# A decoder block in fp32r: stationary operands read with a step of two elements

## The chip, the cores and the metric

The kernel runs on one core of a Trainium2 chip. The metric is the device time of one execution in microseconds. The profiler's record of one execution is read as the page and as answers from the trace; the engines are TensorE (PE, its weight loads PEld), VectorE (DVE), ScalarE (ACT), GpSimd (POOL) and the queue engine SP.

## The reference

One layer on x of 256 tokens by 2048 channels, batch 1:

```python
proj = x @ w_in                       # 2048 -> q, k, v, gates of two branches
o = gla_chunked(q, k, v, log_a)       # gated linear attention, 4 heads
y_gla = (rms(o) * gla_norm_g * silu(gr)) @ w_branch_gla
y_fox = fox_attention(fq, fk, fv, log_f) @ w_branch_fox   # 8 heads
x = layer_norm(ALPHA * x + (sigmoid(ma) * y_gla + sigmoid(mb) * y_fox) @ w_out)
h = gelu(causal_dwconv(x @ w_gate, conv_w, conv_b)) * (x @ w_up)      # 2048 -> 5632
x = layer_norm(ALPHA * x + h @ w_down)
x = x + sigmoid(x @ w_ple_gate) * (p @ w_ple_proj)
```

Everything is float32. The large products are done in fp32r, each from three partial products of a high and a low part.

## The kernel before

**Operands.** Weights come from memory in units of 128 partitions by 2048 floats. `prep` splits each half of a unit: ACT copies it to an fp32r tile `hi` (line 121), DVE subtracts that from the raw values into `lo` (line 241). Activations are kept transposed, channels on partitions, as tiles of four K tiles by 512 columns: 256 columns high part, then 256 low part, each with the 256 tokens in two halves of 128 (`xT`, `x1T`, `x2T`, `oT`, `ofT`, `mC`, `hC`). Sums of activations for Strassen-like products (`xS`, `mS`, `hS`, `gS`) are cells of 128 high and 128 low columns.

**Two kinds of matmul.** In a *weight unit* (`w_unit`, lines 307 and 309; `w_phase`, lines 322 and 326) 128 columns of the weight are stationary and the activation streams: 512 columns against `hi`, then 256 against `lo`. The outputs `psg`, `psu`, `psq` and so on have channels on partitions. Elsewhere 128 tokens of an activation are stationary and 512 columns of weights stream: `fv` (line 472), `x_mm` (line 353), `q_unit` (line 979, for `psm`, `psa`, `psb`), `s_half` (lines 841 and 909, for `gv`, `gr`, `wo`, `dn`, `pg`). Each matmul loads its own stationary operand. `go` (line 1084) multiplies attention weights `ath`, `atl` as stationary by values `vh`, `vl`; transposes use `ident`.

**Order.** Instructions of SP are issued in the written order, and PE's at three places; the rest is ordered by the scheduler from its cost estimates. Weight units are prepared up to three ahead. Side work (attention steps, sums, differences of weights stored for later as `td`) is pulled in between units by generators. SBUF pools are laid out one behind the other, with paddings `GAPS` between them and a shift `LO_SHIFT` of 16 floats of the `lo` tiles in all units outside `UA`; the change leaves these as they are.

Of the kernel before, what the change touches and what calls it, by code (L numbers as in the profile page):

```python
# [78 lines left out]
def tile_block(ctx: ExitStack, tc: tile.TileContext, wu, wfv, wpp, xT_in, x_in, pT_in, wlr,  # L79
# [219 lines left out]

    def w_unit(ps, hi, lo, act, kts, first, last, hoff=0, tick=None):  # L300


        n = len(kts)
        for i, kt in enumerate(kts):
            a = act[kt // 4]
            w0 = (hoff + i) * P
            nc.tensor.matmul(ps, lhsT=hi[i // 8 if hoff == 0 else 0][:, w0 % 1024:w0 % 1024 + P],  # L307
                             rhs=a[:, kt % 4, :], start=first and i == 0, stop=False)
            nc.tensor.matmul(ps[:, 256:512],  # L309
                             lhsT=lo[i // 8 if hoff == 0 else 0][:, w0 % 1024:w0 % 1024 + P],  # L310
                             rhs=a[:, kt % 4, 0:256], start=False, stop=last and i == n - 1)
            if tick is not None:
                tick(i)

    def w_phase(ps, hi, lo, act, t, kts, part=slice(None)):


        p4 = ps.rearrange("p (s t n) -> p s t n", s=2, t=2)
        for kt in kts[part]:
            a = act[kt // 4][:, kt % 4, :]  # L320
            w = slice(kt % 8 * P, kt % 8 * P + P)
            nc.tensor.matmul(p4[:, :, t, :], lhsT=hi[kt // 8][:, w],
                             rhs=a.rearrange("p (s t n) -> p s t n", s=2, t=2)[:, :, t, :],
                             start=t == 0 and kt == kts[0], stop=False)
            if t == 1:
                nc.tensor.matmul(ps[:, 256:512], lhsT=lo[kt // 8][:, w], rhs=a[:, 0:256],
                                 start=False, stop=kt == kts[-1])

    def comb(ps, o, scale=1.0):
        tmp = t1("tmp")  # L330
        copy(tmp, ps[:, 256:512], scale)
        a = ps[:, 0:256]
        if len(o.shape) == 3:
            a, tmp = [v.rearrange("p (t n) -> p t n", t=2) for v in (a, tmp)]
        if scale == 1.0:
            nc.vector.tensor_tensor(o, a, tmp, ALU.add)
        else:
            nc.vector.scalar_tensor_tensor(o, a, scale, tmp, ALU.mult, ALU.add)

    def x_mm(banks, w, a, toks, first, last, cs=(0, 1), part=None):  # L340
# [117 lines left out]
    for u in range(8):  # L458
        hi, lo = fvu[u]
        for j in range(2):  # L460
            kt = 2 * u + j
            a = xT[kt // 4][:, kt % 4, :]
            prods = [[(hi[j], a[:, t * P:t * P + P]), (hi[j], a[:, 256 + t * P:256 + t * P + P]),
                      (lo[j], a[:, t * P:t * P + P])] for t in range(2)]
            if u < 2:
# [118 lines left out]
    def fox_gen():  # L584
# [40 lines left out]
        def values(h):  # L625
# [6 lines left out]
            dst = ofT[h // 4][:, h % 4, :]  # L632
            copy(dst[:, 0:256], po[:, 0:256])
            nc.vector.tensor_tensor(dst[:, 256:512], po[:, 0:256],
                                    dst[:, 0:256].bitcast(F32), ALU.subtract)

# [15 lines left out]
    for n in range(16):  # L652
# [6 lines left out]
        if n % 8 == 0:  # L659
            fqk[h // 4] = s8([P, 4, 2, 256], name=f"fqk{h // 4}")  # L660
        comb(ps, fqk[h // 4][:, h % 4, j], (P ** -0.5, 1.0)[j])
        if n >= 1:
# [124 lines left out]
    def cell(o, i):  # L787

        return o[:, i, 0:P], o[:, i, P:256]

    def s_sums(y):

        a11, a21, a12, a22 = [y[:, k, t * P:t * P + P] for k in range(2) for t in range(2)]
        v = t2("sums").rearrange("p (i t) -> p i t", t=P)
# [5 lines left out]
    def sums(y, name, scale=1.0, full=False):  # L800
# [7 lines left out]
        for e, src in parts:  # L808
            copy(o[:, e, 0:P], src, scale)
            hi = o[:, e, 0:P].bitcast(F32)  # L810
            if scale == 1.0:
                nc.vector.tensor_tensor(o[:, e, P:256], src, hi, ALU.subtract)
            else:
                nc.vector.scalar_tensor_tensor(o[:, e, P:256], src, scale, hi, ALU.mult,
                                               ALU.subtract)
# [110 lines left out]
    def x_sums(pairs):  # L926
        for i, pair in pairs:
# [19 lines left out]
            nc.sync.dma_start(y, xT_in[:, 2 * pair:2 * pair + 2, :])  # L947
            v = s_sums(y)
            for j, w in enumerate(ws):
                src = v[:, j * m:j * m + m]  # L950
                copy(w[:, :, 0:P], src)
                nc.vector.tensor_tensor(w[:, :, P:256], src, w[:, :, 0:P].bitcast(F32),
                                        ALU.subtract)
            yield

    def x_cl(pair, j, t):
        kt = 2 * pair + j
        a = xT[kt // 4][:, kt % 4, :]
        return a[:, t * P:t * P + P], a[:, 256 + t * P:256 + t * P + P]

    def x_st(pair, i):
        if i < 3:
            return x_cl(pair, (0, 1, 1)[i], (0, 0, 1)[i])
        o = xS[pair][i - 3]
        return o[:, 0:P], o[:, P:256]


    def q_unit(ps, act, k, first, last, tick=None):
# [4 lines left out]
        def part(i, t):  # L973
            kt = 4 * k + i
            o = act[kt // 4][:, kt % 4, :]
            ah, al = o[:, t * P:t * P + P], o[:, 256 + t * P:256 + t * P + P]
            h, l = [w[i // 2][:, i % 2 * 512:i % 2 * 512 + 512] for w in (hi, lo)]
# [137 lines left out]

    def split_T(pt, dst, t):

        p3 = pt.rearrange("p (k t) -> p k t", t=P)
        hi = dst[:, :, t * P:t * P + P]
        copy(hi, p3)  # L1120
        nc.vector.tensor_tensor(dst[:, :, 256 + t * P:256 + t * P + P], p3,
                                hi.bitcast(F32), ALU.subtract)

# [18 lines left out]
    def turn_pair(pair):  # L1142
# [19 lines left out]
        nc.vector.scalar_tensor_tensor(dst[:, :, 256:512], p3, 0.5,  # L1162
                                       dst[:, :, 0:256].bitcast(F32), ALU.mult, ALU.subtract)

# [23 lines left out]
    def ln_steps(zof, stats, t, act_out, gb_, cg, cb, nm, prio, aff):  # L1188
# [29 lines left out]
        def turn(g):  # L1218
            zc = zof(t, g)
            with tc.high_priority(prio):  # L1220
# [3 lines left out]
                if g in aff:  # L1224
                    split_T(pt, act_out[g], t)
                    return
                y = t2("lny").rearrange("p (k t) -> p k t", t=P)
                for i in range(4):
# [5 lines left out]
                    else:  # L1234
                        nc.vector.tensor_scalar(y[:, i, :], src, gc, bc, ALU.mult, ALU.add)
                hi = act_out[g][:, :, t * P:t * P + P]
                copy(hi, y)
                nc.vector.tensor_tensor(act_out[g][:, :, 256 + t * P:256 + t * P + P], y,
                                        hi.bitcast(F32), ALU.subtract)

        return stat, norm, turn

    def out_proj(nh, tail, mid, end=None):
        def cl(pair, j, t):
# [3 lines left out]
            a = mC[i // 2][:, i % 2 * 2 + j, :]  # L1248
            return a[:, t * P:t * P + P], a[:, 256 + t * P:256 + t * P + P]

# [169 lines left out]
    for n in range(NF):  # L1420
# [30 lines left out]
        dst = hC[n // 4][:, n % 4, :]  # L1451
        copy(dst[:, 0:256], h)
        nc.vector.tensor_tensor(dst[:, 256:512], h, dst[:, 0:256].bitcast(F32), ALU.subtract)
        if pair in DN_S[0] and j == 1:
            v = s_sums(yp)
            for i in range(2):
                w = sm.tile([P, 2, 256], F32R, tag="t2", bufs=6, name="hs")
                copy(w[:, :, 0:P], v[:, 2 * i:2 * i + 2])
                nc.vector.tensor_tensor(w[:, :, P:256], v[:, 2 * i:2 * i + 2],
                                        w[:, :, 0:P].bitcast(F32), ALU.subtract)  # L1460
                k = DN_S[0].index(pair)
# [26 lines left out]
    def down(nh, tail, mid):  # L1488
        def cl(pair, j, t):
            a = hC[pair // 2][:, pair % 2 * 2 + j, :]  # L1490
            return a[:, t * P:t * P + P], a[:, 256 + t * P:256 + t * P + P]

# [106 lines left out]
    def g_cl(pair, j, t):  # L1599
        kt = 2 * pair + j  # L1600
        a = x2T[kt // 4][:, kt % 4, :]
        return a[:, t * P:t * P + P], a[:, 256 + t * P:256 + t * P + P]

    gS_ = {}

    def g_sums(pairs):
        two = s8([P, 8, 256], F32R, name=f"gS{pairs[0]}")
        for i, pair in enumerate(pairs):
# [3 lines left out]
            nc.vector.tensor_tensor(y, a[:, :, 0:256], a[:, :, 256:512], ALU.add)  # L1612
            v = s_sums(y)
            copy(o[:, :, 0:P], v)
            nc.vector.tensor_tensor(o[:, :, P:256], v, o[:, :, 0:P].bitcast(F32), ALU.subtract)
            gS_[pair] = o
# [38 lines left out]
def _wst(w):  # L1655

    k, n = w.shape
    kt, nt = k // P, n // P
    per = 2048 // (kt * P)
# [32 lines left out]
def _fold(a):  # L1692

    return np.concatenate([a[:P], a[P:][::-1]], 0)


# [4 lines left out]
def _layout(i):  # L1701
# [26 lines left out]
    for lev in range(1, 8):  # L1728
# [4 lines left out]
    cmask = np.concatenate([caus.T, caus], 1)  # L1733
    return dict(wu=wu, wfv=wfv, wpp=_xst(i["w_ple_proj"][0]), xT=x.T.reshape(16, P, S).transpose(1, 0, 2),
                x=x.reshape(2, P, D), pT=_fold(i["p"][0, 0]).T.reshape(2, P, S).transpose(1, 0, 2),
                wlr=i["w_gla_lr"][0], chan=chan, gnorm=i["gla_norm_g"], lng=lng,
# [21 lines left out]
```

## Time and profile before

| | |
|---|---|
| median of 3 runs | 1645.58 us (1645.08 to 1645.61) |
| span of the profiled execution | 1645.0 us |
| PE busy | 1638.4 us, 8,422 matmuls |
| PEld busy | 1404.3 us |
| DVE busy | 1356.0 us, 1,964 instructions |
| ACT busy | 910.3 us, 1,277 instructions |
| moved by DMA | 477.81 MB, 290 GB/s |

The profiled execution has no time of its own beside its span; the runs' median stands 0.6 us above that span. In the page a row of a group reads: line, engine, operation, output<-inputs, shapes, count | busy us, mean ns of one | idle us of the engine before them and what ended it. In a timeline a row is: start in us, duration in us, engine, line, operation, count. In a table of windows it is the busy time of each engine with the number of its instructions, the granted TensorE clock, the busy share of the DMA engines and GB/s. A row of one line's instructions gives count, the minimum, median and maximum of a duration in ns, and the first and last start.

### The profile page before, as it was taken

The numbers are of one execution on the slowest core, as the hardware profiler recorded it, in microseconds if no ns is written. First come the engines' busy times: TensorE is split into PE (matmuls) and PEld (weight loads), VectorE is DVE, ScalarE is ACT, GpSimd is POOL, SyncE is SP. The second block draws the span as 40 slices with busy tenths as digits, with TensorE's granted clock in tenths as the row PEclk, the third lists the DMA queues.
The fourth block names the chain that finished last, engine by engine and source line by source line (L and its number), as shares of the span: only waits on it lengthen the run. The fifth ranks groups of instructions, "written<-read, shape, count | busy, mean of one in ns | idle before, by whom it ended". The sixth has DMA issues, their size and how long they took to land.

```text
span 1645.0 us, 23490 instructions
## 1 busy us (share of the span) xinstructions
PE 1638.4 (100%) x8422; PEld 1404.3 (85%) x8422; DVE 1356.0 (82%) x1964; ACT 910.3 (55%) x1277; POOL 92.7 (6%) x244
## 2 busy tenths in 40 slices
PE   9999999999999999999999999999999999999998
PEld 9988888888888888887898888888888888888887
DVE  7687899788989867778987888887887778988887
ACT  6655555456666654446574445555455456566554
POOL 0000000000000000000010111110111000000000
PEclk9999999999999999999999999999999999999999
DMA  8799799878888768889855898888766679899574
GB/s 324 281 371 341 290 383 356 294 258 309 306 333 307 252 207 303 305 335 364 296 190 194 315 338 320 308 306 304 279 239 217 210 260 336 305 343 348 177 258 157
DMA packets 114838, 477.81 MB, mean 290 GB/s; under 512 B 13032, under 2 KB 14320, under 8 KB 95136
## 3 DMA queue, kind: packets, MB, share of 16 engines
q1 hardware_dynamic: 105216, 417.57, 70.8%
q0 software_dynamic: 9504, 58.73, 8.9%
q8 instruction: 66, 1.08, 0.2%
q14 instruction: 52, 0.43, 0.1%
HBM read 417.53 MB, written 58.73 MB: 290 GB/s over the span
## 4 chain that ended last, share of the span: by engine, by line
PE 97%; DMA 1%; DVE 1%; ACT 0%; issue 0%; POOL 0%; ACTq 0%
PE psm L979 11%; PE dn L841 10%; PE psu L307 10%; PE psg L307 9%; PE psa L979 5%; PE psu L309 5%; PE psg L309 5%; PE dn_p L841 4%; PE gr L841 3%; PE gv L841 3%; PE fv L472 3%; PE pg L353 3%; PE psb L979 3%; PE wo L841 2%; PE gr_p L841 2%; PE gv_p L841 2%
## 5 line engine op out<-in xcount | busy, mean ns | idle before, releaser
L241 DVE TENSOR_TENSOR lo<-raw,hi 128x1024 fp32r<-128x1024 f32 x456 | 551.1, 1220 | 140.7 <-ACT hi L121 139.4
L121 ACT ACTIVATE hi<-raw 128x1024 fp32r<-128x1024 f32 x456 | 476.6, 1057 | 304.2 <-DMA raw<-in_wu_dram 83.7
L307 PE MATMUL psu<-x1T,hi 128*128 128x512 f32 x688 | 240.4, 392 | 0.0
L307 PE MATMUL psg<-x1T,hi 128*128 128x512 f32 x672 | 234.8, 392 | 0.0
L309 PE MATMUL psu<-x1T,lo 128*128 128x256 f32 x688 | 192.3, 280 | 0.0
L309 PE MATMUL psg<-x1T,lo 128*128 128x256 f32 x672 | 187.8, 280 | 0.0
L979 PE MATMUL psm<-hi,xT 128*128 128x512 f32 x512 | 163.0, 392 | 0.0
L307 PEld LDWEIGHTS psu<-x1T,hi 128*128 128x128 f32 x688 | 129.2, 188 | 27.6
L307 PEld LDWEIGHTS psg<-x1T,hi 128*128 128x128 f32 x672 | 126.2, 188 | 27.0
L309 PEld LDWEIGHTS psu<-x1T,lo 128*128 128x128 f32 x688 | 130.6, 190 | 0.0
L121 ACT ACTIVATE hi_b<-raw 128x512 fp32r<-128x512 f32 x112 | 92.9, 841 | 66.8 <-DMA raw<-in_wu_dram 17.9
L309 PEld LDWEIGHTS psg<-x1T,lo 128*128 128x128 f32 x672 | 127.6, 190 | 0.0
L159 DVE TENSOR_TENSOR td<-td 128x512 f32<-128x512 f32 x172 | 117.6, 684 | 0.9
L215 DVE TENSOR_TENSOR lo_b<-raw,hi_b 128x512 fp32r<-128x512 f32 x112 | 104.9, 952 | 15.9 <-ACT hi_b L121 15.6
L979 PEld LDWEIGHTS psm<-hi,xT 128*128 128x128 f32 x512 | 96.2, 188 | 19.6
L215 DVE TENSOR_TENSOR lo_t<-td,hi_t 128x1024 fp32r<-128x1024 f32 x86 | 101.7, 1219 | 12.7 <-ACT hi_t L121 12.0
L121 ACT ACTIVATE hi_t<-td 128x1024 fp32r<-128x1024 f32 x86 | 88.0, 1053 | 28.9 <-DMA td<-td 15.1
L979 PE MATMUL psm<-lo,xT 128*128 128x512 f32 x256 | 99.8, 390 | 0.0
L841 PE MATMUL dn<-hi,hC 128*128 128x512 f32 x352 | 97.8, 389 | 0.0
L979 PE MATMUL psa<-hi,oT 128*128 128x512 f32 x256 | 81.2, 392 | 0.0
L841 PEld LDWEIGHTS dn<-hi,hC 128*128 128x128 f32 x352 | 66.0, 188 | 13.7
L979 PEld LDWEIGHTS psa<-hi,oT 128*128 128x128 f32 x256 | 48.1, 188 | 10.0
(414 smaller groups left out, 3130.8 us busy)
## 6 DMA issues: line engine op xcount, KB each, us to landing
raw<-in_wu_dram SPq DMA_DIRECT2D x525, 512.0 KB, 6.3
td<-in_wu_dram SPq DMA_DIRECT2D x43, 1024.0 KB, 8.8
td<-td POOLq DMA_DIRECT2D x43, 1024.0 KB, 7.7
td<-td SPq DMA_DIRECT2D x43, 1024.0 KB, 8.3
hS<-sd SPq DMA_DIRECT2D x11, 1024.0 KB, 8.8
raw<-in_wu_dram SPq DMA_DIRECT2D x43, 256.0 KB, 7.7
fvraw<-in_wfv_dram SPq DMA_DIRECT2D x13, 524.0 KB, 6.6
sd<-hs POOLq DMA_DIRECT2D x24, 256.0 KB, 5.6
```

The source lines that it names most:

```text
L121: return nc.scalar.activation(o, i, AF.Copy, bias=0.0, scale=scale)
L159: sub = lambda o, a, b: nc.vector.tensor_tensor(o, a, b, ALU.subtract)
L215: nc.vector.tensor_tensor(lo, src, hi.bitcast(F32), ALU.subtract)
L241: i = nc.vector.tensor_tensor(lo, raw, hi.bitcast(F32), ALU.subtract)
L307: nc.tensor.matmul(ps, lhsT=hi[i // 8 if hoff == 0 else 0][:, w0 % 1024:w0 % 1024 + P], rhs=a[:, kt % 4, :], start=first and i == 0, stop= ...
L309: nc.tensor.matmul(ps[:, 256:512], lhsT=lo[i // 8 if hoff == 0 else 0][:, w0 % 1024:w0 % 1024 + P], rhs=a[:, kt % 4, 0:256], start=False, ...
L353: nc.tensor.matmul(bs[j][:, 0:m], lhsT=x, rhs=v[:, o:o + m], start=first and i == 0, stop=last and i == 2)
L472: nc.tensor.matmul(fbk[t][c][:, 0:n], lhsT=x, rhs=w[:, o:o + n], start=kt == 0 and i == 0, stop=kt == 15 and i == 2)
L841: nc.tensor.matmul(ps[:, e], lhsT=x, rhs=w, start=k == 1, stop=k == total.get(id(ps), 3 * ns))
L979: nc.tensor.matmul(ps[t], lhsT=x, rhs=v, start=first and i == 0 and j == 0, stop=last and i == 3 and j == 2)
```

## The change

All fp32r stationary operands but those of `go`, of the gates' low-rank product and of a sum over partitions are read with a step of two elements, 8 bytes. For that, data are laid out anew:

- Weight units: the host writes two K tiles in turn, element by element (`_wst`); `wcols` reads every second column.
- Activations: the two token halves stand in turn, element by element, in the high and in the low part (`tok`, `by_half`). The host does it for `x` and `p` (`_mix`); elsewhere ACT and DVE write with a step of two (`put_T`, `hC`, `mC`, `ofT`). `x1T`, which only streams, keeps its order.
- Cells: the high and the low value of a token stand side by side (`cell`, `cells`).
- Where a tile in the new order streams, its products come out with tokens in that order; `comb` then reads PSUM by halves.
- The split of an `mC` pair is done in two instructions on ACT and two on DVE, not one each.

```diff
+    def tok(a, s, t):
+
+        return a.rearrange("p (s n t) -> p s t n", s=2, t=2)[:, s, t, :]
+
+    def by_half(v):
+
+        return v.rearrange("p (n t) -> p t n", t=2)
...
+    def wcols(w, kt):
+
+        v = w[kt // 8].rearrange("p (k n j) -> p k j n", n=P, j=2)
+        return v[:, kt % 8 // 2, kt % 2, :]
...
-            nc.tensor.matmul(ps, lhsT=hi[i // 8 if hoff == 0 else 0][:, w0 % 1024:w0 % 1024 + P],
-                             rhs=a[:, kt % 4, :], start=first and i == 0, stop=False)
...
+            nc.tensor.matmul(ps, lhsT=wcols(hi, i), rhs=a[:, kt % 4, :],
+                             start=first and i == 0, stop=False)
+            nc.tensor.matmul(ps[:, 256:512], lhsT=wcols(lo, i), rhs=a[:, kt % 4, 0:256],
+                             start=False, stop=last and i == n - 1)
...
-            a, tmp = [v.rearrange("p (t n) -> p t n", t=2) for v in (a, tmp)]
+            a, tmp = by_half(a), by_half(tmp)
...
-            ah = a[:, t * P:t * P + P]
-            al = a[:, 256 + t * P:256 + t * P + P]
+            ah, al = tok(a, 0, t), tok(a, 1, t)
...
     def cell(o, i):
 
-        return o[:, i, 0:P], o[:, i, P:256]
...
+        v = o[:, i, :].rearrange("p (n j) -> p j n", j=2)
+        return v[:, 0, :], v[:, 1, :]
...
+    def put_T(src, dst, t, mixed):
+
+        if mixed:
+            hi, lo = [dst.rearrange("p k (s n t) -> p s t k n", s=2, t=2)[:, i, t] for i in range(2)]
+        else:
+            hi, lo = [dst[:, :, o + t * P:o + t * P + P] for o in (0, 256)]
+        copy(hi, src)
+        nc.vector.tensor_tensor(lo, src, hi.bitcast(F32), ALU.subtract)
...
-        dst = mC[i // 2][:, i % 2 * 2:i % 2 * 2 + 2, :]
-        copy(dst[:, :, 0:256], p3, 0.5)
-        nc.vector.scalar_tensor_tensor(dst[:, :, 256:512], p3, 0.5,
-                                       dst[:, :, 0:256].bitcast(F32), ALU.mult, ALU.subtract)
+        for k in range(2):
+            dst = mC[i // 2][:, i % 2 * 2 + k, :]
+            hi, lo = by_half(dst[:, 0:256]), by_half(dst[:, 256:512])
+            src = p3[:, k, :].rearrange("p (t n) -> p t n", t=2)
+            copy(hi, src, 0.5)
+            nc.vector.scalar_tensor_tensor(lo, src, 0.5, hi.bitcast(F32), ALU.mult, ALU.subtract)
...
-    a = w.reshape(kt, P, nt // per, per, P).transpose(2, 1, 3, 0, 4)
-    return a.reshape(nt // per, P, 2048)
+    a = w.reshape(k // 256, 2, P, n // P, P).transpose(3, 2, 0, 4, 1)
+    return a.reshape(n // P, P, k)
...
+def _mix(a):
+
+    return a.reshape(-1, 2, P).transpose(0, 2, 1).reshape(a.shape)
```

The numbers of instructions on PE, POOL and SP stay; DVE and ACT have three more each. Order changes at one place, the start of `wo`. ACT before (`mC` from the turned tiles `mt` of pairs 6 and 7, among the splits of unit 122):

```order
L121 ACTIVATE hi122_b2_6991<-raw122_1_6982 128x1024
L121 ACTIVATE mC0_6213<-mt6_7027 128x2x256
L121 ACTIVATE mC1_7039<-mt7_7034 128x2x256
L121 ACTIVATE hi122_t13_6995<-td122_6985 128x1024
L121 ACTIVATE hi122_t24_6999<-td122_6985 128x1024
```

ACT now:

```order
L129 ACTIVATE hi122_b2_6993<-raw122_1_6984 128x1024
L129 ACTIVATE mC0_6213<-mt6_7029 128x2x128
L129 ACTIVATE mC1_7043<-mt7_7038 128x2x128
L129 ACTIVATE hi122_t13_6997<-td122_6987 128x1024
L129 ACTIVATE mC0_6213<-mt6_7029 128x2x128
L129 ACTIVATE hi122_t24_7001<-td122_6987 128x1024
L129 ACTIVATE mC1_7043<-mt7_7038 128x2x128
```

The second halves of the two splits stand behind the copies of unit 122. PE before (products p5, p7, p6 of unit 121, one row of three each; p6 and p7 take the two banks that `mt` and other turned tiles use):

```order
L841 MATMUL wo0_p5_6980<-hi121_t13_6928,mS1_6269 128x512
L841 MATMUL wo0_p7_7067<-hi121_t13_6928,mS1_6269 128x512
L841 MATMUL wo0_p7_7067<-lo121_t13_6929,mS1_6269 128x512
L841 MATMUL wo0_p7_7067<-hi121_t13_6928,mS1_6269 128x512
L841 MATMUL wo0_p6_7066<-hi121_t24_6932,mS1_6269 128x512
L841 MATMUL wo0_p6_7066<-lo121_t24_6933,mS1_6269 128x512
L841 MATMUL wo0_p6_7066<-hi121_t24_6932,mS1_6269 128x512
L841 MATMUL wo0_10_6977<-hi121_t24_6932,mS1_6269 128x512
```

PE now, from the last of unit 121's other products on:

```order
L858 MATMUL wo0_10_6979<-hi121_t24_6934,mS1_6271 128x512
L858 MATMUL wo0_p1_6981<-hi122_b11_6989,mS3_6551 128x512
L858 MATMUL wo0_p1_6981<-lo122_b11_6990,mS3_6551 128x512
L858 MATMUL wo0_p1_6981<-hi122_b11_6989,mS3_6551 128x512
L858 MATMUL wo0_00_6977<-hi122_b2_6993,mS3_6551 128x512
L858 MATMUL wo0_00_6977<-lo122_b2_6994,mS3_6551 128x512
L858 MATMUL wo0_00_6977<-hi122_b2_6993,mS3_6551 128x512
L858 MATMUL wo0_01_6978<-hi122_b2_6993,mS3_6551 128x512
L858 MATMUL wo0_p7_7073<-hi121_t13_6930,mS1_6271 128x512
L858 MATMUL wo0_p7_7073<-lo121_t13_6931,mS1_6271 128x512
```

The six matmuls of p7 and p6 of unit 121 now stand behind seven matmuls of unit 122, and, with them, three of product 10 that need other banks.

More of the change, by code (lines that the diff above doesn't have):

```diff
@@ L297, in load_consts2, with w_unit @@
             nc.gpsimd.tensor_copy(mask[:, 4 * i:4 * i + 4, :], maskf)
-    def w_unit(ps, hi, lo, act, kts, first, last, hoff=0, tick=None):
+    def wcols(w, kt):
+        v = w[kt // 8].rearrange("p (k n j) -> p k j n", n=P, j=2)
+        return v[:, kt % 8 // 2, kt % 2, :]
+    def w_unit(ps, hi, lo, act, kts, first, last, tick=None):
         n = len(kts)
@@ L462, in tile_block @@
             a = xT[kt // 4][:, kt % 4, :]
-            prods = [[(hi[j], a[:, t * P:t * P + P]), (hi[j], a[:, 256 + t * P:256 + t * P + P]),
-                      (lo[j], a[:, t * P:t * P + P])] for t in range(2)]
+            prods = [[(hi[j], tok(a, 0, t)), (hi[j], tok(a, 1, t)), (lo[j], tok(a, 0, t))]
+                     for t in range(2)]
             if u < 2:
@@ L787, in cell, with cells, s_sums @@
     def cell(o, i):
-        return o[:, i, 0:P], o[:, i, P:256]
-    def s_sums(y):
-        a11, a21, a12, a22 = [y[:, k, t * P:t * P + P] for k in range(2) for t in range(2)]
+        v = o[:, i, :].rearrange("p (n j) -> p j n", j=2)
+        return v[:, 0, :], v[:, 1, :]
+    def cells(o):
+        v = o.rearrange("p i (n j) -> p j i n", j=2)
+        return v[:, 0], v[:, 1]
+    def s_sums(y, mixed=False):
+        h = y.rearrange("p k (n t) -> p k t n" if mixed else "p k (t n) -> p k t n", t=2)
+        a11, a21, a12, a22 = [h[:, k, t] for k in range(2) for t in range(2)]
         v = t2("sums").rearrange("p (i t) -> p i t", t=P)
@@ L1601, in g_cl @@
         a = x2T[kt // 4][:, kt % 4, :]
[L1602 removed]
+        return tok(a, 0, t), tok(a, 1, t)
     gS_ = {}
```

86 lines of the change are left out of this document (38 added, 48 removed).

## The prediction

> **What bounds the kernel now.** I read the page first: busy times, granted clock, the chain that ended last.
>
> ```profile
> span 1645.0 us, 23490 instructions
> PE 1638.4 (100%) x8422; PEld 1404.3 (85%) x8422; DVE 1356.0 (82%) x1964; ACT 910.3 (55%) x1277; POOL 92.7 (6%) x244
> ...
> PEclk9999999999999999999999999999999999999999
> ...
> PE 97%; DMA 1%; DVE 1%; ACT 0%; issue 0%; POOL 0%; ACTq 0%
> ```
>
> The reader is to see that TensorE never lacks work at a full granted clock. The list of waits, for PE alone, confirms it; this is its whole answer:
>
> ```profile
> PE warm_ps L131 <- DVE warm L128: 1.2, 1, 1.2
> PE wo L841 <- DVE lo_b L215: 0.4, 1, 0.4
> PE wo_p L841 <- ACT hi_t L121: 0.2, 1, 0.2
> ```
>
> So the time is what 8,422 matmuls take back to back, and the question is what one costs. A matmul's own record overlaps the next one's, so I take distances between starts, from the timeline of PE. First the gate units, which alternate 512 and 256 columns (first rows, and the row twelve pairs later):
>
> ```profile
> 999.81 0.28 PE L309 MATMUL psg<-x1T,lo 128*128 128x256 f32 x1
> 999.93 0.39 PE L307 MATMUL psg<-x1T,hi 128*128 128x512 f32 x1
> ...
> 1003.97 0.28 PE L309 MATMUL psg<-x1T,lo 128*128 128x256 f32 x1
> ```
>
> 4.16 us / 12 = 346.7 ns a pair. Then a merge gate, 512 columns only (first row, and the row twelve matmuls later):
>
> ```profile
> 300.21 0.39 PE L979 MATMUL psm<-lo,xT 128*128 128x512 f32 x1
> ...
> 302.93 0.39 PE L979 MATMUL psm<-lo,xT 128*128 128x512 f32 x1
> ```
>
> 2.72 / 12 = 226.7 ns. The 256-column matmul therefore takes 346.7 - 226.7 = 120.0 ns, so 256 more columns cost 106.7 ns, 0.4167 ns each; 512 columns stream in 213.3 ns, and **13.3 ns of every matmul do not depend on its columns**. That is the sum at stake. A third place has the same form, 512 columns, with stationary and moving operands from other tiles (first row, and the row six matmuls later):
>
> ```profile
> 584.39 0.39 PE L1084 MATMUL go<-vh,ath 128*128 128x512 f32 x1
> ...
> 585.79 0.39 PE L1084 MATMUL go<-vh,ath 128*128 128x512 f32 x1
> ```
>
> 1.40 / 6 = 233.3 ns: here the surplus is 20.0 ns. Same type, same columns, same clock; what differs is where the operands lie. In the kernel's own allocation the next stationary starts 256 bytes (modulo 512) past the moving operand in nearly all 512-column matmuls, and 320 bytes past it in these. So at least 6.7 ns of such a surplus belong to the addresses that the weight load and the stream read at the same time.
>
> **The change, part by part.** Of the matmuls, 8,010 get a stationary with step two (counted in the built program); the 251 fp32 ones, the 36 of `go` and 16 others keep step one. Columns, count, DMAs and SP's and POOL's rows stay.
>
> (1) The load and the stream. The stream covers 4 bytes in 0.4167 ns, 9.6 bytes/ns. The load's own rate is seen where nothing else limits it, in transposes of 128 columns:
>
> ```profile
> 552.97 1.03 PE L1102 MATMUL gt<-ident,og 128*128 128x128 f32 x8
> ...
> L1102 PE MATMUL gt<-ident,og 128*128 128x128 f32 x32 | 4.1, 272 | 0.0
> L307 PEld LDWEIGHTS psg<-x1T,hi 128*128 128x128 f32 x672 | 126.2, 188 | 27.0
> L309 PEld LDWEIGHTS psg<-x1T,lo 128*128 128x128 f32 x672 | 127.6, 190 | 0.0
> ```
>
> (1.03 - 0.272) / 7 = 108 ns for 128 columns, 4.7 bytes/ns with step one: half the stream's pace. So the stream overtakes the load once in a while, and if both come to the same part of the memory, one must wait. With step two the load walks at 9.5 bytes/ns, the stream's pace: a distance that is free of meetings at the start stays free. The trace has no load with step two, so the gain is bounded: above by the whole 13.3 ns (8,010 x 13.3 = 106.8 us), below by nothing or a loss (rivals). The nearest row is that of `go`: 6.7 ns hang on addresses there, 53.4 us if that much goes. I take the middle of 6.7 and 13.3, 10 ns, since the usual placement may still contain meetings that no placement with step one avoids: **-80.1 us**. [...]
>
> (2) VectorE and ScalarE write and read activations with step two. Line 718 has steps of two elements at its lowest level (one of seven) and runs at the others, so its spread holds the price; line 728 is plain, and line 713 is the same case on ACT:
>
> ```profile
> L718 DVE TENSOR_TENSOR kq<-gk,e x28: 408/416/426, 188.0 to 365.3; 128x256 f32<-128x256 f32 x28
> ...
> L728 DVE TENSOR_TENSOR kq<-gq,e 128x256 f32<-128x256 f32 x4 | 1.7, 417 | 0.0
> ...
> L713 ACT ACTIVATE e<-e x28: 399/418/449, 186.9 to 364.5; 128x256 f32<-128x256 f32 x28
> ```
>
> 416 against 417 ns on DVE, and at most 31 ns over the median on ACT: nothing that counts from SBUF. Reading PSUM with step two (32 combines of q and k) is not in the trace; between nothing and a doubling of this row's 419 ns (13 us of DVE in all) I take nothing, as the SBUF rows do, and keep 5 us for the range, since DVE idles little there:
>
> ```profile
> L338 DVE SCALAR_TENSOR_TENSOR gq<-psq,tmp 128x256 f32<-128x256 f32 x8 | 3.4, 419 | 3.2 <-ACT tmp L121 3.2
> ```
>
> (3) Three `mC` splits become six. On DVE 683 ns become 2 x 419 (the row above has the half size), half a microsecond in all; ACT is as little. But at the start of `wo` ACT's second halves now stand behind two `hi_t` copies:
>
> ```profile
> L1162 DVE SCALAR_TENSOR_TENSOR mC<-mt,mC x3: 680/683/683, 651.1 to 747.1; 128x512 fp32r<-128x512 f32 x3
> ...
> 745.24 1.07 ACT L121 ACTIVATE mC<-mt 128x512 fp32r<-128x512 f32 x2
> 746.20 2.07 ACT L121 ACTIVATE hi_t<-td 128x1024 fp32r<-128x1024 f32 x2
> ```
>
> The bank that `mt` holds comes free about 2 us later, and products p6 and p7 wait for such a bank. PE has seven matmuls moved ahead of them (7 x 0.227 = 1.6 us) as cover. Between 0 and 2 us; I take **+1**.
>
> (4) What a faster TensorE runs into. DVE, ACT and DMA keep their work; in 41-us windows:
>
> ```profile
> core 0: us, PE busy (x) PEld busy (x) DVE busy (x) ACT busy (x) POOL busy (x), PEclk, DMA share, GB/s
> 82.00:123.00 41.00, 41.00 (x243) 36.47 (x242) 36.61 (x66) 22.06 (x42) 2.13 (x4) 1.00 0.99 372
> 205.00:246.00 41.00, 41.00 (x247) 36.58 (x246) 38.91 (x63) 20.23 (x32) 2.13 (x4) 1.00 0.99 387
> 738.00:779.00 41.00, 40.32 (x180) 32.45 (x179) 36.48 (x41) 27.12 (x32) 0.53 (x1) 1.00 0.98 367
> 779.00:820.00 41.00, 41.00 (x182) 33.95 (x181) 39.42 (x48) 21.60 (x22) 0.53 (x1) 1.00 0.85 310
> ...
> L241 DVE TENSOR_TENSOR lo<-raw,hi 128x1024 fp32r<-128x1024 f32 x456 | 551.1, 1220 | 140.7 <-ACT hi L121 139.4
> ```
>
> At 5% less, a window has 39 us. Three have DMA at 0.98 or more: if none of them shrinks, 3 x 2 = 6 us come back. In the last one DVE alone needs 39.4 us, and its splits also wait for ACT; I give such windows 4 us. Late next are thus the splits and the transfers: **+10**.
>
> **Sum.** 1645.0 - 80.1 + 1 + 10 = 1575.9 us of span; the runs' median, 1645.58, stands 0.6 above the span. So 1576.5, rounded to 1577.
>
> **Rivals.**
> (a) *No effect.* The 13.3 ns are a fixed turn of the array from one stationary to the next, and step one and two load alike: 1646. Against it: 233.3 beside 226.7 ns. For it: only a placement was varied there, never the step. [...]
> (b) *More meetings, slower.* A load with step two covers 1,024 bytes instead of 512. If each stretch that it reads costs the stream as much as now, the surplus doubles: 8,010 x 13.3 = +107, 1752. It decides as soon as the surplus passes 13.3 ns; lockstep helps only where the distance happens to be good, and the placements were left as they were.
> (c) *The load itself slows.* Behind a 256-column matmul it has 120 ns and needs 108; past 120 ns the 2,052 matmuls of 256 columns start to wait. At twice the time, 216 ns, 2,052 x 96 = +197: 1843. The 512-column ones (226.7) still hide it. No row shows a strided load. [...]
> (d) *Given back.* The matmuls gain as said or a third of it, and splits and transfers hold the rest: 1600 to 1640. DVE at 82% of the span (87% of 1576) speaks against a general stall.
>
> **How the numbers follow.** Forecast 0.55, its own range 1555 to 1602 (gains of 13.3 and 6.7 ns, 10 to 18 us given back); (d) 0.09; (a) 0.11; (b), fully or in part, 0.15; (c) 0.10. That is 0.64 faster by over 0.2%, 0.11 within it (about what a measurement of this kernel can tell from no change), 0.25 slower. A range for 8 in 10 starts at 1553 and leaves out (c) and the larger half of (b): 1690 is about 6 ns more per matmul.
>
> **What would show it.** Right: 512-column starts 215 to 220 ns apart in `psm`, pairs of the gate units 320 to 332, and `go`, which keeps step one, still at 233; DVE over 85% of the span. (a): 226.7 and 346.7 unchanged. (b): 512 and 256 both longer by the same amount. (c): 512 unchanged, 256 well above 120, a longer PEld record than 188 ns. (d): the distances shrink, yet PE shows waits for `hi`, `lo` and `raw`. The prediction is wrong if the meetings are not what the surplus is made of, or if lockstep holds the two readers together instead of apart.

## The result, and the profile after

The changed kernel takes 1680.98 us (median; 1680.64 to 1681.37) against 1645.33 us (1644.32 to 1645.61) for the kernel before in the same comparison: a ratio of 1.0216, 95% interval 1.0201 to 1.023. It is slower; the forecast was faster.

From the page of the kernel after, span, busy times, granted clock and the chain that ended last:

```profile
span 1679.2 us, 23499 instructions
PE 1673.5 (100%) x8422; PEld 1444.4 (86%) x8422; DVE 1359.9 (81%) x1967; ACT 914.7 (54%) x1280; POOL 93.6 (6%) x244
...
PEclk9999999999999999999999999999999999999999
...
PE 99%; DMA 0%; ACT 0%; DVE 0%; SPq 0%; issue 0%; POOL 0%; POOLq 0%
```

The list of PE's waits is one row, at the start:

```profile
PE warm_ps L139 <- DVE warm L136: 1.2, 1, 1.2
```

The bound is what it was: 8,422 matmuls back to back at full clock (1.000 granted), now without a wait behind the first one. PE's busy time and the span grew by nearly the same amount (35.1 and 34.2 us), so the matmuls themselves cost more. PE's timeline of after, a start and a later one of the same kind: gate units (12 pairs apart), the merge gate (30 matmuls apart), `go` (six apart; the end row is the next stage's first), and the transposes:

```profile
999.74 0.28 PE L321 MATMUL psg<-x1T,lo 128*128 128x256 f32 x1
1003.98 0.28 PE L321 MATMUL psu<-x1T,lo 128*128 128x256 f32 x1
...
302.51 0.39 PE L996 MATMUL psm<-lo,xT 128*128 128x512 f32 x1
309.51 0.39 PE L996 MATMUL psm<-lo,xT 128*128 128x512 f32 x1
...
596.51 0.39 PE L1101 MATMUL go<-vh,ath 128*128 128x512 f32 x1
597.91 0.40 PE L996 MATMUL psm<-hi,xT 128*128 128x512 f32 x1
...
563.82 1.04 PE L1119 MATMUL gt<-ident,og 128*128 128x128 f32 x8
```

A pair takes 4.24 / 12 = 353.3 ns (before 346.7), a 512-column matmul of `psm` 7.00 / 30 = 233.3 ns (before 226.7). `go`, which keeps step one, stays at 1.40 / 6 = 233.3, and the transposes at (1.04 - 0.272) / 7 = 110. Summed over start-to-start distances, weight-unit matmuls went from 670.4 to 682.3 us (+12.0), those with activations stationary from 928.8 to 951.1 (+22.3), all others stayed at 40.0: together the growth of the span. In a pair of the gate units most of it stands behind the 512-column half: 229.6 to 235.0 ns on the mean; behind the 256-column half it is 117.1 to 118.3.

So the surplus over the columns' time, 13.3 ns in `psm`, became 20.0, the value that `go` had before. The columns' time, 213.3 ns for 512, is the prediction's estimate from 0.4167 ns a column; `steps` below gives (226.7 - 120.7) / 256 = 0.414 with step one. The question for the experiments: is that the price of step two, or of step two at these addresses?

### The profile page after: what moved, and what is told of

It reads as the page before. It is cut to its first block, busy times and chain, and to the rows that moved or that the text cites. A ratio compares the mean times of both kernels' runs of the same rounds, so it can differ in the third digit from the quotient of the medians.

```text
span 1679.2 us, 23499 instructions
## 1 busy us (share of the span) xinstructions
PE 1673.5 (100%) x8422; PEld 1444.4 (86%) x8422; DVE 1359.9 (81%) x1967; ACT 914.7 (54%) x1280; POOL 93.6 (6%) x244
## 4 chain that ended last, share of the span: by engine, by line
PE 99%; DMA 0%; ACT 0%; DVE 0%; SPq 0%; issue 0%; POOL 0%; POOLq 0%
PE psm L996 11%; PE dn L858 10%; PE psu L319 10%; PE psg L319 9%; PE psa L996 5%; PE psu L321 5%; PE psg L321 5%; PE wo L858 4%; PE dn_p L858 4%; PE gv L858 3%; PE gr L858 3%; PE pg L362 3%; PE psb L996 3%; PE fv L481 2%; PE gr_p L858 2%; PE gv_p L858 2%
## 5 line engine op out<-in xcount | busy, mean ns | idle before, releaser
L319 PE MATMUL psu<-x1T,hi 128*128 128x512 f32 x688 | 245.0, 397 | 0.0
L319 PE MATMUL psg<-x1T,hi 128*128 128x512 f32 x672 | 239.3, 397 | 0.0
L319 PEld LDWEIGHTS psu<-x1T,hi 128*128 128x128 f32 x688 | 134.3, 195 | 25.4
L319 PEld LDWEIGHTS psg<-x1T,hi 128*128 128x128 f32 x672 | 131.2, 195 | 24.9
L321 PEld LDWEIGHTS psu<-x1T,lo 128*128 128x128 f32 x688 | 136.5, 198 | 0.0
L321 PEld LDWEIGHTS psg<-x1T,lo 128*128 128x128 f32 x672 | 133.3, 198 | 0.0
L223 DVE TENSOR_TENSOR lo_b<-raw,hi_b 128x512 fp32r<-128x512 f32 x112 | 105.5, 953 | 22.3 <-ACT hi_b L129 22.0
L167 DVE TENSOR_TENSOR td<-td 128x512 f32<-128x512 f32 x172 | 117.9, 685 | 0.9
```

What stands on the lines that cost most here:

```text
L167: sub = lambda o, a, b: nc.vector.tensor_tensor(o, a, b, ALU.subtract)
L223: nc.vector.tensor_tensor(lo, src, hi.bitcast(F32), ALU.subtract)
L319: nc.tensor.matmul(ps, lhsT=wcols(hi, i), rhs=a[:, kt % 4, :], start=first and i == 0, stop=False)
L321: nc.tensor.matmul(ps[:, 256:512], lhsT=wcols(lo, i), rhs=a[:, kt % 4, 0:256], start=False, stop=last and i == n - 1)
```

## The experiments

**Each half of the change alone.** `weights_only` puts the change's `wcols` and `_wst` into the kernel before; `acts_only` takes them out of the kernel after.

```diff
-            nc.tensor.matmul(ps, lhsT=hi[i // 8 if hoff == 0 else 0][:, w0 % 1024:w0 % 1024 + P],
+            nc.tensor.matmul(ps, lhsT=wcols(hi, i), rhs=a[:, kt % 4, :],
```

> Step two for the weight units alone, activations as before. In the trace of the changed kernel the matmuls of these units took 12.0 us more than before and the others 22.3 us more. If the cost is local to the matmul whose load is strided: 1645 + 12 = 1657 us. If the strided activations disturb all matmuls (through slower writes by the other engines): nearer to 1646 us.

> Step two for the activations and cells alone, weight units as before. If the cost is local to the matmul whose load is strided: 1645 + 22 = 1667 us, with the weight units' pairs back at 347 ns. If the strided writes of the other engines carry it: nearer to 1681 us.

Measured: 1657.13 us (1.0065, 1.0048 to 1.0082) and 1669.47 us (1.014, 1.0125 to 1.0155), beside 1646.09 before. 11.0 and 23.4 us add to 34.4, close to the whole change's 35.7, and near the forecasts for a cost that is local to the matmul (1657 and 1667). PE's timelines, twelve pairs of `weights_only` and then 18 matmuls of `acts_only`:

```profile
1000.10 0.28 PE L313 MATMUL psu<-x1T,lo 128*128 128x256 f32 x1
...
1004.34 0.28 PE L313 MATMUL psg<-x1T,lo 128*128 128x256 f32 x1
```

```profile
302.44 0.39 PE L994 MATMUL psm<-lo,xT 128*128 128x512 f32 x1
...
306.64 0.39 PE L994 MATMUL psm<-lo,xT 128*128 128x512 f32 x1
```

353.3 and 233.3 ns, as in the whole change. The halves act apart and each on its own matmuls; strided writes by DVE and ACT are only in `acts_only`, and there too the matmul spacing accounts for the time.

**Streams: step against distance.** `steps` computes nothing of the block. Each case is 24 equal matmuls, the next load meant to run under the current stream, as in the kernel before (there the load for a `psm` matmul on `hi` starts at 300.21 us, with the matmul on `lo`, and its own matmul at 300.43); the distance is that from the moving operand to the stationary one.

```python
nc.tensor.matmul(ps[:, 0:n], lhsT=view(sta, off, [(step, 128)]), rhs=view(mov, 0, [(j, n)]),
                 start=i == 0, stop=i == 23)
```

> This kernel computes none of the block: it streams 24 fp32r matmuls per case, one stationary operand loaded again for each, and varies only where the stationary operand lies and the step with which it is read; the other engines rest. Distance is the byte distance from the moving operand to the next stationary one, 0 to 448. Theory 'more stretches': a load with step two touches twice as many short stretches of memory and each disturbs the stream; then 512 columns take about 226.7 ns with step one and about 233.3 ns with step two at every distance, step three and four take more again (some 240 and 247 ns), and beyond the step at which each element lies in a stretch of its own nothing more is added. Rival 'placement': the placement was good for step one only; then step two has distances at 220 ns or less and others at 233 ns or more, and step one varies by distance as well (226.7 at 256, 233.3 at 320). Rival 'longer load': the load takes longer and the surplus depends on neither the distance nor the step beyond two; then 256 columns, with 120 ns to hide a load in, suffer more than 512.

PE's timeline of `steps`; names are step and distance in bytes, written in letters (a = 0 to j = 9: `cfg` 256, `dca` 320, `die` 384); `movtwo` reads the moving operand with step two, `bf` is bf16. The distance between the starts of successive rows, divided by 24, is one matmul:

```profile
60.86 5.62 PE L46 MATMUL one_cfg__283<-mov,sta 128*128 128x512 f32 x24
66.32 5.76 PE L46 MATMUL one_dca__308<-mov,sta 128*128 128x512 f32 x24
71.92 5.74 PE L46 MATMUL one_die__333<-mov,sta 128*128 128x512 f32 x24
...
121.99 5.76 PE L46 MATMUL two_cfg__558<-mov,sta 128*128 128x512 f32 x24
127.59 5.68 PE L46 MATMUL two_dca__583<-mov,sta 128*128 128x512 f32 x24
...
179.25 10.99 PE L46 MATMUL movtwo_one__808<-mov,sta 128*128 128x512 f32 x24
190.06 11.11 PE L46 MATMUL movtwo_two__833<-mov,sta 128*128 128x512 f32 x24
...
230.47 5.36 PE L46 MATMUL bf_b__1033<-mob,stb 128*128 128x512 bf16 x24
235.66 5.34 PE L46 MATMUL bf_c__1058<-mob,stb 128*128 128x512 bf16 x24
```

Step one at 256 bytes takes 5.46 / 24 = 227.5 ns with the change-over between groups (226.7 without it), at 320 bytes 5.60 / 24 = 233.3: these are `psm` and `go` of the kernel before, reproduced. Step two at 256 bytes takes 233.3: `psm` of after. So neither DMA nor the other engines nor the order is needed for it. bf16 takes 216.2 ns with step one and 215.8 with step two, a surplus of 2.5 to 2.9 over 213.3. None of the three theories came out whole: step two is not at 233.3 everywhere (230 at 64 and at 320 bytes), no distance brings it to 220, and 256 columns take 120.7 with step one and 119.5 with step two. Steps of 3, 4, 5, 8 and 12 elements at 256 bytes take 235.6, 235.2, 236.7, 246.6 and 268.3 ns.

**Every distance, and the load by itself.** `fine` repeats this at every 16 bytes over 256 bytes, and adds 128-column matmuls, whose columns take an estimated 53 ns (128 x 0.4167), so that the load should be the limit.

> Again no block, only streams of 24 equal matmuls: distances in steps of 16 bytes over 256 bytes, for step one and step two at 512 columns; four distances at 256 columns; and 128 columns with steps 1, 2, 3, 4 and 8, where the load itself must be the limit. Theory 'distance and step': the surplus of a 512-column matmul depends on the distance modulo 256 bytes with both steps, between 226.7 and 233.5 ns for step one and between 229.8 and 233.4 for step two, so that step two has no distance as good as step one's best. Rival 'lockstep, only misplaced': among the finer distances step two has some at 220 ns or less. Rival 'longer load': at 128 columns step two needs clearly more than the 109 ns of step one; by the theory it needs 109 as well, and step 4 and 8 about 230.

Step one: 226.7 ns once settled (the first few starts of a group can differ) at 0, 16 and 240 bytes, 228.9 and 229.8 on the mean at 192 and 176, 232 to 234 at the other eleven. Step two: from 230.0 (at 112, with 230.3 at 64) to 233.5, nowhere less. Lockstep should have brought some distance to 220 or less; there is none. The timeline of the 128-column groups, `load_b`, `_c`, `_d`, `_e`, `_i` with steps 1, 2, 3, 4, 8:

```profile
228.00 2.79 PE L46 MATMUL load_b__1133<-mov,sta 128*128 128x128 f32 x24
230.63 2.99 PE L46 MATMUL load_c__1158<-mov,sta 128*128 128x128 f32 x24
233.46 4.33 PE L46 MATMUL load_d__1183<-mov,sta 128*128 128x128 f32 x24
237.62 5.81 PE L46 MATMUL load_e__1208<-mov,sta 128*128 128x128 f32 x24
243.22 5.96 PE L46 MATMUL load_i__1233<-mov,sta 128*128 128x128 f32 x24
```

One of these matmuls takes 2.63 / 24 = 110 ns with step one, 118 with two, 173 with three, 233 with four. Only the step of the load differs, so I read them as the load's own times; the theory had 109 for step two, so here it failed. At step two such a load, 118 ns, still fits under 120 ns of a 256-column stream, and streams of 256 columns alone take 119.7 to 120.7 ns, beside 117.9 to 119.2 with step one.

**A smaller load.** `columns` keeps 512 moving columns and cuts the stationary operand to 96, 64, 32 and 16 columns.

> Streams only, none of the block. First the number of stationary columns is cut (128, 96, 64, 32, 16) with 512 moving columns, for both steps, at distances 0 and 64. If the surplus is what the load's reads take from the stream, it falls with the columns: from 32 array cycles (13.3 ns) to about 16 (6.7 ns) or less at 32 columns for step one at distance 0, and with step two from 48 towards the same value, so that the two steps differ little at 32 columns. If it is a fixed cost of changing the stationary operand, it stays at 32 and 48 cycles whatever the columns. Then two streams in turn, as in the weight units (512 and 256 columns) and as in the activation units (512 and 512), over a grid of distances with step one: if some pair of distances is below the 346.7 ns, or below 453.3 ns for two of 512, that the kernel before reaches, a placement with step one is still better than both kernels; I expect none better by more than 2 ns.

Step two at distance 0, 128 and 16 stationary columns, then at distance 64, 64 columns (first and next row of each):

```profile
78.26 5.76 PE L46 MATMUL cols_two_a_bci__358<-mov,sta 128*128 128x512 f32 x24
83.86 5.70 PE L46 MATMUL cols_two_a_jg__383<-mov,sta 128*96 128x512 f32 x24
...
100.56 5.73 PE L46 MATMUL cols_two_a_bg__458<-mov,sta 128*16 128x512 f32 x24
106.13 5.68 PE L46 MATMUL cols_two_ge_bci__483<-mov,sta 128*128 128x512 f32 x24
...
117.10 5.60 PE L46 MATMUL cols_two_ge_ge__533<-mov,sta 128*64 128x512 f32 x24
122.54 5.71 PE L46 MATMUL cols_two_ge_dc__558<-mov,sta 128*32 128x512 f32 x24
```

At distance 0 it is 233.3 and 5.57 / 24 = 232.1 ns: an eighth of the load, nearly the same surplus (20.0 and 18.8 ns). With step one there the smaller load is even dearer (226.7 ns for 128 columns, 231.7 for 16). At distance 64 step two takes 230.0 ns for 128 columns, 227.1 for 96, 5.44 / 24 = 226.7 for 64, then 231.2 for 32 and 231.7 for 16: the number of columns matters, but not in one direction. If the surplus were made of load reads that hold up the stream, each at a price, it would fall with their number. It doesn't, so that account falls, in both directions; a wait that comes once for each matmul is not excluded.

The run also has pairs of 512 and 256 columns with step one, and there the forecast (no placement better than the kernel's 346.7 ns by more than 2) missed: one pair of distances takes 340.0.

**The same paddings for both kernels.** `after_moved` and `before_moved` change only the paddings of the pools, so that activations lie 64 bytes (modulo 256) from the weights they multiply.

```diff
-GAPS = (96, 64, 80)
+GAPS = (80, 80, 80)
...
-LO_SHIFT = 16
+LO_SHIFT = 32
```

> The changed kernel with the paddings between the pools set so that the next stationary activation lies 64 bytes (modulo 256) past the moving weights, not 0; the distance of the weight units' 512-column streams stays 64. Theory 'distance and step': 3,675 matmuls go from 233.4 to about 230.0 ns, -12.5 us, 1668 us. Rival 'more stretches, whatever the distance': 1681 us. Rival 'lockstep, only misplaced': well below 1645 us.

> The kernel before, step one, with the same new paddings. Theory 'distance and step': the 3,675 matmuls go from 227.0 to about 233.3 ns, +23 us, 1668 us: at this placement the two steps cost the same or step two less. Rival 'more stretches, whatever the distance': stays at 1646 us, since only the number of stretches counts.

Measured: after 1666.72 us (1.0126, 1.0109 to 1.0143), before 1668.42 us (1.0135, 1.012 to 1.015), both close to the forecast 1668, with 1646.12 for the unmoved kernel before. PE's timelines, 12 matmuls of `psm` in `after_moved`, then in `before_moved`:

```profile
300.57 0.39 PE L996 MATMUL psm<-lo,xT 128*128 128x512 f32 x1
...
303.33 0.39 PE L996 MATMUL psm<-lo,xT 128*128 128x512 f32 x1
```

```profile
300.05 0.39 PE L979 MATMUL psm<-lo,xT 128*128 128x512 f32 x1
...
302.85 0.39 PE L979 MATMUL psm<-lo,xT 128*128 128x512 f32 x1
```

2.76 / 12 = 230.0 with step two, 2.80 / 12 = 233.3 with step one: at this placement step two is the faster one in the matmuls with activations stationary. In the gate units it is the slower one (351.1 ns a pair, 346.7 with step one), so that the kernels are level. 14 of the change's 35.7 us come back by padding, without a change of step.

**All placements.** `grid` runs pairs (512 and 256 columns) and triples (high, low, high weights moving, as in `psm`) over the two distances involved, for both steps. A cell of pairs is named by the distances of the high operand, which loads under the 256-column stream, and of the low one, which loads under the 512-column stream (in the kernel before, the load of `hi` starts at 1000.16 us, beside the 256-column matmul of 1000.15, and that of `lo` at 1000.27, with the 512-column one): by `GAPS` and `LO_SHIFT` the kernel before and the changed one stand at (0, 64), modulo 256 bytes.

> Streams only. The weight units' pair (512 columns, then 256) with step one over all distances in steps of 16 bytes, with step two in steps of 32; the activation units' triple (high weights, low weights, high weights, 512 columns each) with both steps in steps of 32. Theory 'start of a matmul': the surplus is the wait of a matmul for its turn after the stationary operand changes, between about 24 and 48 array cycles (10 and 20 ns) by distances, step and columns together, with no floor of 32; then step one has its best pair at 340 ns or a little under and step two some pair near 345 ns too, and triples lie between 665 and 700 ns with both steps. Rival 'step two always costs more': its best pair and its best triple stay above 350 and 690 ns.

The first and second triple cell (both distances 0, then 0 and 32), first with step one, then with step two, and the group behind them all; a cell is 9 triples:

```profile
1141.81 6.29 PE L64 MATMUL tripled_a_a__6828<-mov,sta 128*128 128x512 f32 x27
1147.94 6.40 PE L64 MATMUL tripled_a_dc__6856<-mov,sta 128*128 128x512 f32 x27
...
1542.39 6.46 PE L64 MATMUL tritwo_a_a__8620<-mov,sta 128*128 128x512 f32 x27
1548.69 6.46 PE L64 MATMUL tritwo_a_dc__8648<-mov,sta 128*128 128x512 f32 x27
...
1943.56 5.35 PE L46 MATMUL bf_b__10412<-mob,stb 128*128 128x512 bf16 x24
```

Over 64 placements a triple takes (1542.39 - 1141.81) / 576 = 695.5 ns with step one and (1943.56 - 1542.39) / 576 = 696.5 with step two: alike. The cell of the kernel before, (0, 0), takes 6.13 / 9 = 681 with step one (680.0 once settled, the lowest of the 64; the highest is 706.7) and 6.30 / 9 = 700.0 with step two (lowest 686.7). That is 20 ns a triple, 6.7 ns a matmul, beside 6.2 on the mean of these matmuls in the kernel. The forecast that some triples come near 665 failed. The pair cell (0, 64), first with step one, then with step two (first rows of the cell and of the next):

```profile
35.73 0.39 PE L54 MATMUL pair_a_ge__192<-mov,sta 128*128 128x512 f32 x1
...
39.20 0.40 PE L54 MATMUL pair_a_ia__213<-mov,sta 128*128 128x512 f32 x1
...
923.14 0.39 PE L54 MATMUL two_a_ge__5526<-mov,sta 128*128 128x512 f32 x1
...
926.68 0.39 PE L54 MATMUL two_a_jg__5547<-mov,sta 128*128 128x512 f32 x1
```

3.47 / 10 = 347 and 3.54 / 10 = 354 ns: the 346.7 and 353.3 of the two kernels, so the loss of the weight units is reproduced as well. For pairs step two is dearer on the mean (352.7 against 349.3) and at best (346.7 against 340.0). But a cell of pairs is not a fixed number: with step one (64, 0) takes 340.0 ns in `columns` and 349.7 in `grid`, and (192, 0) takes 350.0 and 340.1.

**Using the grid.** Three kernels take placements from it. `after_best` gives the changed kernel other paddings (`GAPS` 80, 32, 80, a gap of 48 floats between the pools of `hi` and `lo`, `LO_SHIFT` 0). `hi_shifted` and `hi_shifted_192` are the kernel before with the high instead of the low tiles of weight units shifted, by 64 and by 192 bytes:

```diff
-        return rlo.tile([P, 1152], F32R, tag="lo", name=f"lo{name}")[:, o:o + 1024]
+        return rlo.tile([P, 1024], F32R, tag="lo", name=f"lo{name}")
+    def hi_tile(u, name):
+        o = HI_SHIFT if u < 32 or 136 <= u < 224 else 0
+        return rhi.tile([P, 1088], F32R, tag="hi", name=f"hi{name}")[:, o:o + 1024]
```

> The changed kernel, step two, with paddings so that the activation units' loads stand 64 bytes past the high and 128 bytes past the low weights, where the grid had its best triple for step two (686.7 ns, against 700.0 at the changed kernel's own 0 and 0), and the weight units' pair at 192 and 128 (349.6 in the grid, some 354 now). If placement is most of the loss: 1,229 triples x 13.3 = -16 us and 1,872 pairs x 4 = -8 us, about 1657 us. If step two itself is most of it: above 1670 us.

> The kernel before (step one) with the shift of 64 bytes given to the high tiles of the weight units and taken from the low tiles: the load under the 512-column stream then stands at distance 0 and the one under the 256-column stream at 64. By the measured grid the pair goes from 346.5 to 340.0 ns: 1,872 x 6.5 = -12.2 us, 1634 us. Rival 'only a stream by itself shows that': a block's real mixture gives 1646 us.

> The kernel before (step one) with the high tiles of the weight units shifted by 192 bytes and the low ones not: distances 192 under the 256-column stream and 0 under the 512-column one, 340.0 ns a pair in the grid but 350.0 in the run before it, whose tiles lay elsewhere. If the distance alone decides: -12 us, 1634 us. If what is beside it (the tiles' other addresses, how a stream began) decides as well: between 1645 and 1655 us.

`after_best`: 1667.27 us (1.0129, 1.0114 to 1.0144), 10 above its forecast: pairs of the gate units take 350.0 ns (349.6 was forecast), but the 512-column matmuls of activations about 231 and not the 228.9 of theirs. `hi_shifted`: 1654.6 us (1.0044, 1.003 to 1.0058), some 20 above its forecast: at (64, 0) all its gate units take 4.24 / 12 = 353.3 ns a pair, not 340.

```profile
1000.10 0.28 PE L312 MATMUL psu<-x1T,lo 128*128 128x256 f32 x1
...
1004.34 0.28 PE L312 MATMUL psg<-x1T,lo 128*128 128x256 f32 x1
```

`hi_shifted_192`: 1638.18 us (0.9967, 0.9947 to 0.9987), so a little faster than both kernels, but of eight runs five lie between 1636.86 and 1638.29 and three between 1645.7 and 1648.79. The profile is of one of the three. PE's timeline, twelve pairs before and twelve after 939.3 us:

```profile
935.20 0.28 PE L312 MATMUL psu<-x1T,lo 128*128 128x256 f32 x1
...
939.28 0.28 PE L312 MATMUL psg<-x1T,lo 128*128 128x256 f32 x1
939.63 0.28 PE L312 MATMUL psg<-x1T,lo 128*128 128x256 f32 x1
...
943.83 0.28 PE L312 MATMUL psg<-x1T,lo 128*128 128x256 f32 x1
```

340.0 ns a pair up to 939.28, 350.0 from 939.63, at unchanged distances, and the new period lasts through all the gate units that follow: 1,086 pairs at 10 ns more are 10.9 us, about what parts the two groups of runs (8 to 11 us). What the other seven runs did in these units is not shown. The distance alone does not fix the period.

**The way in.** `kicks` puts one matmul of 256 + 2k columns, k = 0 to 7, ahead of each group of 16 matmuls or pairs; pairs walk through their tiles as in a weight unit.

> Streams alone; nothing of the block is computed. Ahead of each group of 16 equal matmuls (or 16 pairs of 512 and 256 columns, walking as a weight unit does) stands one matmul of 256 + 2k columns, k = 0 to 7, which shifts the start of the group by 0.83 ns times k. In the run with the high weights shifted by 192 bytes, pairs of one kernel at one distance took 340.0 ns up to the middle of the gate units and 350.0 ns from there on. Theory A (placement and phase: the period that a stream settles in depends on the distance and on how it was entered): within one case at least some groups settle at periods several ns apart, above all step one with distances (0, 192): 340 and 350; step two at distances (64, 0): 345 to 359. Theory B (the distance alone decides, and the two periods came from other traffic on the memory): the eight groups of a case agree within 1 ns. Under both, 512 columns at distance 0: if no entry brings step two to 228 or less while step one stays at 227, the 6.7 ns that the change costs there belong to step and placement, not to phase; if some entry does, they belong to phase.

Its timeline, first the kicks ahead of pairs with step one at the distances (64, 0) of `hi_shifted`, then those ahead of 512 columns with step two at distance 0. The distance from one row to the next is a group of 16 and its kick:

```profile
108.53 0.28 PE L48 MATMUL kick_f__587<-mov,hi 128*128 128x266 f32 x1
114.30 0.28 PE L48 MATMUL kick_g__622<-mov,hi 128*128 128x268 f32 x1
119.86 0.29 PE L48 MATMUL kick_h__657<-mov,hi 128*128 128x270 f32 x1
...
236.50 0.29 PE L48 MATMUL kick_f__1347<-mov,hi 128*128 128x266 f32 x1
240.36 0.29 PE L48 MATMUL kick_g__1366<-mov,hi 128*128 128x268 f32 x1
```

The group behind `kick_g` is 0.21 us shorter than that behind `kick_f`: its pairs settle at 340.0 ns, the other's at 353.3. With step one and (64, 0) the eight groups settle at 340.0 (two), 350.0 (three) and 353.3 (three), so the 353.3 of `hi_shifted` is one of the periods of its placement; at (0, 0) at 346.7 or about 353; at (0, 192) at 346.6 to 351.9, not at 340. With step two, 22 of the 24 groups of pairs settle near 353 and the others at 346.6 and 350.1. Neither the (0, 64) of the two kernels nor the (192, 0) of `hi_shifted_192` is among the three placements. For 512 columns at distance 0 (3.86 us for the group behind `kick_f`) the way in hardly matters: step one settles at 226.6 to 228.1, step two at 233.3 to 233.4 in all eight groups. At distance 64 with step two one group of eight took 233.3 on the mean and the others 230.1 to 230.9. So theory A holds for pairs with step one, theory B for 512 columns alone at distance 0, and the 6.7 ns there belong to step and placement.

## Why the prediction was wrong, point by point

- *What bounds the kernel* held: TensorE, back to back, at full clock. So did the surplus of 13.3 ns per matmul on the mean of a pair. Its split did not: the prediction gave the 512 columns of a pair the 226.7 ns of `psm` and the 256 columns 120.0, but in the pairs before they take 229.6 and 117.1. The 256 bytes "in nearly all 512-column matmuls" hold for those with activations stationary; in the 1,872 of the weight units `LO_SHIFT` puts the low operand, which loads under them, 64 bytes further.
- *Step (1), the load and the stream*, forecast -80.1 us, measured +34.3 (12.0 and 22.3). It is the step that failed, and in its mechanism: it took the surplus for meetings of load and stream that a load at the stream's pace avoids, 10 ns a matmul. That the two meet, and that one then waits, is an assumption of the prediction that no run shows. The runs showed 6.7 ns more instead (233.3 beside 226.7 at the kernel's placement); `columns` shows nearly the same surplus with an eighth of the load at distance 0 (18.8 beside 20.0 ns), and `fine` no distance at which step two comes below 230 ns with 128 columns. It also read the pair 226.7 and 233.3 in one direction only, as a cost that could be taken away. 226.7 was the best case: `psm` sat at one of three distances in sixteen, and at the lowest triple of 64, and after the change sits at 700.0 a triple, in the dearer third for step two.
- *Step (2)*, strided writes at nothing, held: combining q from PSUM takes 420 ns (419 before), writing `hC` 420 and 421 (419 before), and the sum of matmul spacings leaves nothing over. *Step (3)*, +1 us at the start of `wo`: not seen; PE's list of waits holds the first matmul alone. *Step (4)*, +10 us given back, fell away with the gain.
- *Rival (b), slower*, had the sign and, in its own sentence that the placements were left as they were, the place. The sign came out, but not for its reason: its price was wrong (+107 for a doubled surplus; the surplus grew by half in `psm`), and so were its mechanism and the mark set for it (512 and 256 longer by the same): 512 grew by 5.4 ns in the pairs and by 6.7 in `psm`, 256 by 1.2.
- *Rival (c), a slower load*: a load of 118 ns instead of 110 is real (`fine`, as read there), and so is its mark of a longer PEld record (195 and 198 ns in the gate units, 188 and 190 before), but it stays below the 120 ns from which it was to cost, and the 512-column matmuls lost most. *Rival (a), no effect*: refuted for this kernel, though over all placements of a triple (695.5 and 696.5) it is nearly right. *Rival (d)* had nothing to give back.
- What stays open: what makes the surplus. It depends on the step and the distance, in pairs also on the way in, and settled periods are mostly multiples of 3.33 ns (226.7, 230.0, 233.3, 340.0, 346.7, 350.0, 353.3). The runs don't show whether a unit waits, and which, what chooses one of the periods, nor why the activations of `after_best` missed their cell; triples were tried with one way in only.

## What to carry to other kernels

When two groups of the same form differ in the trace only by where their operands lie (here 226.7 and 233.3 ns), the faster one is at risk as much as the slower one is a chance: before changing an access pattern, ask where in the spread of placements the rows stand that carry the time, and test pattern and placement together. A stream of equal matmuls over a grid of distances gives that spread in one run; compare patterns by their means and by their best cells, not at the placement that one of them happens to have. A placement found so is to be tried in the kernel, since what a pair settled at here also depended on how it was entered (340.0 to 353.3 ns at one placement in `kicks`).

## What the runs showed of the hardware, unexpected

- With step one or two, fp32r matmuls of 512 columns that each load a stationary operand took 226.7 to 234 ns in `fine` with 128 stationary columns, and 231.7 to 232.1 in `columns` with 16: 13 to 21 ns more than the 213.3 estimated for the columns. In bf16 they took 215.8 and 216.2 (`steps`), 2.5 to 2.9 more.
- Pairs settled in one of several lasting periods at the same distances: 340.0 and 350.0 ns within one execution of `hi_shifted_192`, whose eight runs spread over 12 us.
- Matmuls of 128 stationary and 128 moving columns took 110, 118, 173 and 233 ns with steps 1, 2, 3 and 4 in the stationary operand (`fine`). With step two in the moving operand, matmuls of 512 columns took (190.06 - 179.25) / 24 = 450 ns instead of 227.5 (`steps`).
